# Loans of PSUM banks eight ticks apart, copies inside the next product, and another rule for ordering ScalarE, VectorE and GpSimd in a two-layer decoder

## Chip, core and metric

One core of a Trainium2 chip runs the whole program. The metric is the device time of one execution in microseconds (us). Engines are named as the profile names them: PE is TensorE (PEld its weight loads), DVE is VectorE, ACT is ScalarE, POOL is GpSimd, SP is SyncE, which issues most DMAs.

## What is computed

The reference runs 512 positions of width 1024, in float32, through two layers; each is followed by `x <- LayerNorm(alpha * x + sublayer(x))`.

```python
# even layer: one input projection feeds two branches
q, k, v, g_ret, xb, g_lru = split(x @ w_in)
ret = groupnorm(retention(rope(q), rope(k), v)) * silu(g_ret)     # 8 heads, chunks of 128
lru = rg_lru(conv4(xb)) * silu(g_lru)                             # gates, scan over positions
y = concat(ret, lru) @ w_out
# odd layer: differential attention, 8 heads, value width 256
q, k, v, g = split(x @ w_in)
w = softmax(q1 k1) - lam * softmax(q2 k2)                         # causal
y = (rmsnorm(w @ v) * silu(g)) @ w_out
```

## The kernel before

**Precision.** Each float32 operand of a product is split into a high part and a low remainder: ACT casts the high part, DVE subtracts it (`split`, L152 and L153). A product is then three matmuls, high by high (L156), low by high (L158) and high by low (L159), into one PSUM bank. So each weight tile of 128x1024 costs one ACT cast (`w53h`) and one DVE subtraction (`w53l`) behind its load; in the profile `w_r` is the raw tile.

**Stages.** The even layer's units run in the order of a list: gates (`gl`, `gr`), LRU inputs (`xb`), `q` and `k` per head, values (`ev`), and output products (`out`, `lo`, `ro`, `eo`) that add into `y` on DVE (L260, L262). `q` and `k` go through `rope`: three multiplications out of PSUM (L346, L349, L350), a sum (L351) and a split. Retention then multiplies keys by queries (`rs`), weights the scores (`rsd`, L475), multiplies by values (`ro`), and normalises (`rq`, `rv`, L497 to L508) into `retm`. The LRU branch goes through gate products (`pr`, `pi`), ACT functions with table loads (L528 to L544) and DVE rows up to a scan (L548) and L551 (`xc`), into `lrum`. At the end of the layer each block of 128 rows is normalised (`bst`, L371; L390, L392) and transposed on PE (`ht`, L615), and `hh` and `hl` are its two parts.

The odd layer computes values and gates of later groups together (`gates_values`): seven products of half blocks, some with weights and activations summed beforehand (`sx`), into two pairs of banks, `one` (`gv..a`) and `two` (`gv..b`). Between the products the banks are copied to SBUF (`p1`, `u`, `p7`).

**Order.** PE and SP keep the order of the code (`manual_schedule`). ACT, DVE and POOL are ordered by the scheduler from its own simulation of the program, with priorities given in the code (`high_priority(P_...)`). The side work, an attention block or a retention head, is a Python generator that is stepped by a clock, `side`: each call of `side.tick()`, after three matmuls of a main product, lets at most one such job go a step. A job yields the number of ticks to wait or a function that tells when. So the ticks set where the transposes (`wt`, L670), value products (`po`) and output transposes (L698) of an attention block stand in PE's order.

**Banks.** PSUM has four banks for main products (`ps_pj`), two for scores (`ps_sc`), one for `po` (`ps_av`) and one for transposes. An attention block takes `ps_av` for its value product, from there to the transposes of its result, plus `ATT_FREE` ticks. During `qk` units (`spare[0]` is true) it always borrows a bank of `ps_pj` instead, without a limit. The result `o` (L694) needs a square sum of `po` on ACT (L688) and a reciprocal root on POOL (L691, L363).

Of the kernel before, what the change touches and what calls it, by code (L numbers as in the profile page):

```python
# [34 lines left out]
ATT_TURN = (4, 3, 4, 4)  # L35
ATT_NORM = 5
ATT_VALUE, GV_VALUE = 2, 4
ATT_FREE = 2

P_ROPE, P_SCORES, P_SQUARE, P_GROUP, P_VALUE = 50, 13, 60, 5, 60  # L40
P_CONV, P_GATES = 9, 5
# [62 lines left out]
def trunk(ctx: ExitStack, tc: tile.TileContext, a):  # L104
    nc = tc.nc
    PS = bass.MemoryType.PSUM

    def pool(name, bufs, stack=ctx, **kw):
        return stack.enter_context(tc.tile_pool(name=name, bufs=bufs, **kw))
# [15 lines left out]
    side = Side()  # L125
    ALL = slice(None)

    def work(name):
        return wk.tile([P, S], F32, tag="wk", name=name)
# [4 lines left out]
    def bank(pl, tag, name):  # L134
        return pl.tile([P, 512], F32, tag=tag, name=name)
# [136 lines left out]
    for p in range(3):  # L272
        one, two = (2 * p, 2 * p + 1)
# [5 lines left out]
    for kind, i in ev:  # L279
        if kind in ("ro", "lo", "out"):  # L280
            order += [(eo[2 * i + j + n], None) for n in {"ro": (0,), "lo": (8,), "out": (8, 0)}[kind] for j in range(2)]
        else:
            n = 4 if kind == "v" else 1
# [9 lines left out]
    for kind, i in od:  # L293
        if kind == "o":
            order += [(oo[2 * hd + j], j) for hd in i for j in range(2)]
        elif kind == "gv":
# [3 lines left out]
            t = {n: [dram.tile([P, D], F32, tag=f"t{i}{n}{j}", name=f"t{i}{n}{j}") for j in range(2)] for n in (1, 2, 3, 4)}  # L300
# [104 lines left out]
    two = pool("two", 2, phase)  # L405
# [165 lines left out]
    for kind, i in ev:  # L571
# [18 lines left out]
        else:  # L590
            ps = t_unit(x, f"{kind}{i}")
# [53 lines left out]
    def attention(hd, qb, q, k, m):  # L645
        hc = (hd % 2) * 2 * P
        n = (qb + 1) * P
        ee = []
        z = small.tile([P, 2], F32, tag="z", name="z")
        for mp in range(2):  # L650
            ps = bank(ps_sc, "sc", f"as{hd}{mp}{qb}")
            mm3(ps[:, :n], cut(q[mp], ALL, slice(qb * P, qb * P + P)), cut(k[mp], ALL, slice(0, n)), True, True)
            with tc.high_priority(P_ATT):
                nm = small.tile([P, 1], F32, tag="nm", name="nm")
                nc.vector.tensor_tensor_reduce(out=ps[:, :n], in0=ps[:, :n], in1=mask[:, S - n:], scale=-QK_SCALE, scalar=3.0e38,  # L655
                                               op0=ALU.add, op1=ALU.min, accum_out=nm)
                e = es.tile([P, n], F32, tag=f"e{n}", name=f"e{hd}{mp}{qb}")
                nc.scalar.activation(out=e, in_=ps[:, :n], func=AF.Exp, scale=-1.0, bias=nm, accum_out=z[:, mp:mp + 1])  # L658
            ee.append(e)
        with tc.high_priority(P_ATT):  # L660

            zr = small.tile([P, 2], F32, tag="zr", name="zr")
            nc.vector.reciprocal(out=zr[:, 0:1], in_=z[:, 1:2])
            nc.vector.tensor_scalar(out=zr[:, 0:1], in0=zr[:, 0:1], scalar1=z[:, 0:1], scalar2=nlam, op0=ALU.mult, op1=ALU.mult)
            nc.gpsimd.tensor_scalar(out=zr[:, 1:2], in0=z[:, 0:1], scalar1=z[:, 0:1], scalar2=EPS, op0=ALU.mult, op1=ALU.mult)  # L665
            nc.vector.scalar_tensor_tensor(out=ee[0], in0=ee[1], scalar=zr[:, 0:1], in1=ee[0], op0=ALU.mult, op1=ALU.add)  # L666
        yield ATT_SCORES[qb] + busy[0]
        pt = bank(ps_tp, "tp", f"wt{hd}{qb}")
        for kb in range(qb + 1):
            nc.tensor.transpose(out=pt[:, kb * P:kb * P + P], in_=ee[0][:, kb * P:kb * P + P], identity=ident)  # L670
        with tc.high_priority(P_ATT):
            wt = part(n, f"w{hd}{qb}")
            split(pt[:, :n], wt)
        yield ATT_TURN[qb] + busy[0]

        here = lambda: max(vt.get(hd // 2, math.inf), 0 if spare[0] else av[0])
        if here() > side.now:
            yield here
        own = not spare[0]
        if own:  # L680
            av[0] = math.inf
        v = vs[hd // 2]
        po = bank(*(ps_av, "av") if own else (ps_pj, "pj"), f"po{hd}{qb}")
        for kb in range(qb + 1):
            mm3(po[:, :2 * P], cut(wt, ALL, slice(kb * P, kb * P + P)), cut(v[kb], ALL, slice(hc, hc + 2 * P)), kb == 0, kb == qb)
        with tc.high_priority(P_ATT):
            ss = small.tile([P, 1], F32, tag="ss", name="ss")
            nc.scalar.activation(out=po[:, 2 * P:], in_=po[:, :2 * P], func=AF.Square, scale=(2 * P) ** -0.5, accum_out=ss)  # L688
            rs = small.tile([P, 1], F32, tag="ars", name="ars")
            ve = small.tile([P, 1], F32, tag="rs", name="ave")  # L690
            nc.gpsimd.tensor_scalar(out=ve, in0=ss, scalar1=zr[:, 1:2], scalar2=None, op0=ALU.add)  # L691
            rsqrt(ve, rs)
            o = es.tile([P, 2 * P], F32, tag="o", name=f"o{hd}{qb}")
            nc.vector.scalar_tensor_tensor(out=o, in0=po[:, :2 * P], scalar=rs, in1=gates[qb, hd // 2][:, hc:hc + 2 * P], op0=ALU.mult, op1=ALU.mult)  # L694
        yield ATT_NORM + (not own)
        pm = po[:, 2 * P:]
        for i in range(2):
            nc.tensor.transpose(out=pm[:, i * P:i * P + P], in_=o[:, i * P:i * P + P], identity=ident)  # L698
        with tc.high_priority(P_ATT):
            split(pm.rearrange("p (i s) -> p i s", s=P), cut(m, ALL, ALL, slice(qb * P, qb * P + P)))  # L700

        if own:
            av[0] = side.now + ATT_FREE

    oj, om, vs, vt, av = {}, {}, {}, {}, [0]
# [59 lines left out]
    def load_sum(n, k):  # L765
        for j in range(2):
            nc.sync.dma_start(out=sx[:, k, :, 2 * j:2 * j + 2].bitcast(F32), in_=sd[n][:, :, 2 * j:2 * j + 2])
# [6 lines left out]
    def gates_values(i):  # L774
        def block(r, c):
            return lambda kt, n: cut(h, ALL, 4 * c + kt, slice((2 * r + n) * P, (2 * r + n) * P + P))

        def total(k):
            return lambda kt, n: tuple(sx[:, k, x, kt, n * P:n * P + P] for x in range(2))

        def product(ps, left, start, then=()):
            for j in range(2):
                if j and then:
                    load_sum(*then)
                w = take(3)
                for n in range(2):
                    for kt in range(2 * j, 2 * j + 2):
                        c = kt % 2 * HALF
                        mm3(ps[n], left(kt, n), cut(w, ALL, slice(c, c + HALF)), start and kt == 0, kt == KT // 2 - 1, skip_group_check=not start)
                        side.tick()  # L790

        def copies(ps, name):
            ts = [work(f"{name}{i}{n}") for n in range(2)]
            for t, p in zip(ts, ps):
                nc.scalar.copy(out=t, in_=p)
            return ts

        def gate(ps, ts, r):
            g = gp.tile([P, 2, S], F32, tag="g", name=f"og{i}{r}")
            for n in range(2):  # L800
                for hd in (2 * i - 2, 2 * i - 1):
                    side.need(oj[hd, 2 * r + n])
                gates[2 * r + n, i] = g[:, n]
            for n in range(2):
                nc.vector.tensor_tensor(out=g[:, n], in0=ps[n], in1=ts[n], op=ALU.add)
                silu2(g[:, n], g[:, n], ts[n])

        busy[0] = ATT_BUSY
        one = [bank(ps_pj, "pj", f"gv{i}a{n}") for n in range(2)]
        two = [bank(ps_pj, "pj", f"gv{i}b{n}") for n in range(2)]  # L810
        product(one, block(0, 0), True)
        p1 = copies(one, "p1")
        product(two, block(0, 1), True)
        gate(two, p1, 0)
        product(one, total(0), False)
        u = copies(one, "u")
        product(two, total(1), True, (0, 0))
        p7 = copies(two, "p7")
        product(one, total(0), False, (3, 1))
        past(i - 1)  # L820
        low = []
        for n in range(2):
            nc.vector.scalar_tensor_tensor(out=p7[n], in0=one[n], scalar=-1.0, in1=p7[n], op0=ALU.mult, op1=ALU.subtract)
            low.append(pair(vp, [P, S], "v", f"ov{i}{2 + n}"))
            split(p7[n], low[n])
        product(two, block(1, 1), False)
        gate(two, u, 1)
        product(one, total(1), False)
        for n in range(2):
            t = pair(vp, [P, S], "v", f"ov{i}{n}")  # L830
            nc.scalar.activation(out=t[0], in_=one[n], func=AF.Identity, scale=-1.0)
            nc.vector.scalar_tensor_tensor(out=t[1], in0=one[n], scalar=-1.0, in1=t[0].bitcast(F32), op0=ALU.mult, op1=ALU.subtract)
            vs.setdefault(i, []).append(t)
        vs[i] += low
        vt[i] = side.now + GV_VALUE
        busy[0] = 0
# [8 lines left out]
                for qb in range(SB):  # L845
                    side.need(oj[hd, qb])

    later, units, busy, spare = {}, 0, [0], [False]

    def swap_in():  # L850
        nonlocal sx
# [151 lines left out]
```

## Time and profile before

| | us |
|---|---|
| median of 3 runs | 929.88 |
| lowest to highest | 929.85 to 930.24 |
| profiled execution | 929.83 |
| its span, first to last instruction | 928.1 |
| PE busy in the span | 907.5 |
| DVE busy | 744.1 |
| ACT busy | 478.8 |

The profile gives each row of a timeline as start, duration, engine, line, operation, output and inputs with the buffer numbers left out, shapes, and in brackets the idle time of the engine before it with what ended it. The list of waits gives who waited for whom, the total, how often, and the longest. In the list of stages a row is a window in us, its length, the busy time of PE, PEld, DVE, ACT and POOL with the number of instructions, then the granted share of PE's clock, the DMA share and GB/s. The even layer runs to about 450 us, the odd layer from there.

### The profile page before, as it was taken

The numbers are of one execution on the slowest core, as the hardware profiler recorded it, in microseconds if no ns is written. First come the engines' busy times: TensorE is split into PE (matmuls) and PEld (weight loads), VectorE is DVE, ScalarE is ACT, GpSimd is POOL, SyncE is SP. The second block draws the span as 40 slices with busy tenths as digits, with TensorE's granted clock in tenths as the row PEclk, the third lists the DMA queues.
The fourth block names the chain that finished last, engine by engine and source line by source line (L and its number), as shares of the span: only waits on it lengthen the run. The fifth ranks groups of instructions, "written<-read, shape, count | busy, mean of one in ns | idle before, by whom it ended". The sixth has DMA issues, their size and how long they took to land.

```text
span 928.1 us, 11816 instructions
## 1 busy us (share of the span) xinstructions
PE 907.5 (98%) x4257; PEld 751.7 (81%) x4257; DVE 744.1 (80%) x1244; ACT 478.8 (52%) x779; POOL 103.0 (11%) x167
## 2 busy tenths in 40 slices
PE   9999999999999999999999999999999999999996
PEld 6888888887888878888888888888788888787885
DVE  5887987969768989897888997669867588877787
ACT  5467787556474668532434466333555334563340
POOL 0110010110101010010101120100200101101022
PEclk9999999999999999999999999999999999999998
DMA  7995463962929281525932127555247382286102
GB/s 250 295 295 148 127 180 91 273 171 66 284 61 278 82 206 63 192 87 176 342 130 70 65 79 261 204 204 182 91 133 270 123 293 90 69 274 242 52 1 90
DMA packets 46522, 152.92 MB, mean 165 GB/s; under 512 B 6144, under 2 KB 6272, under 8 KB 45696
## 3 DMA queue, kind: packets, MB, share of 16 engines
q1 hardware_dynamic: 41472, 135.39, 41.3%
q0 software_dynamic: 4992, 16.78, 9.3%
q8 instruction: 33, 0.54, 0.2%
q14 instruction: 25, 0.20, 0.1%
HBM read 139.57 MB, written 37.75 MB: 191 GB/s over the span
## 4 chain that ended last, share of the span: by engine, by line
PE 76%; DVE 13%; ACT 4%; issue 3%; POOL 2%; DMA 1%; SPq 0%; DVEq 0%; POOLq 0%; ACTq 0%
PE oo_ps L159 2%; PE oo_ps L156 2%; PE oo_ps L158 2%; PE out_ps L156 2%; PE out_ps L159 2%; PE out_ps L158 2%; PE gr_ps L159 1%; PE gr_ps L158 1%; PE gr_ps L156 1%; PE gl_ps L156 1%; PE gl_ps L159 1%; PE gl_ps L158 1%; PE xb_ps L158 1%; PE xb_ps L159 1%; PE xb_ps L156 1%
## 5 line engine op out<-in xcount | busy, mean ns | idle before, releaser
L658 ACT ACTIVATE e<-as,nm 128x128 f32<-128x128 f32 (+3 forms) x64 | 33.2, 524 | 39.6 <-DVE nm L655 39.5
L665 POOL TENSOR_SCALAR zr<-z 128x1 f32<-128x1 f32 x32 | 16.5, 516 | 272.0 <-ACT e L658 272.0
L694 DVE SCALAR_TENSOR_TENSOR o<-po,ars,og 128x256 f32<-128x256 f32 x32 | 15.5, 484 | 33.5 <-POOL ars L363 33.4
L187 POOL DMA_DIRECT2D t<-t x24 | 18.9, 786 | 156.0 <-DMA t<-in_od_w 151.0
L187 POOL DMA_DIRECT2D t<-in_od_w x24 | 19.1, 795 | 149.2 <-DMA t<-in_od_w 149.2
L655 DVE CUSTOM_DVE_ANT_0 as<-as,mask 128x128 f32<-128x128 f32 (+3 forms) x64 | 30.4, 508 | 2.2 <-PE as L159 2.0
L691 POOL TENSOR_SCALAR ave<-ss,zr 128x1 f32<-128x1 f32 x32 | 14.5, 454 | 126.3 <-ACT po L688 124.4
L688 ACT ACTIVATE po<-po 128x256 f32<-128x256 f32 x32 | 12.0, 375 | 27.1 <-PE po L159 24.7
L363 POOL TENSOR_TENSOR ars<-ave,nhalf 128x1 f32<-128x1 f32 x32 | 19.5, 610 | 2.7
L536 DVE TENSOR_TENSOR xbp<-xbp,xc 128x512 f32<-128x512 f32 x8 | 5.5, 692 | 17.6 <-ACT xbp L533 17.6
L666 DVE SCALAR_TENSOR_TENSOR e<-e,zr,e 128x128 f32<-128x128 f32 (+3 forms) x32 | 17.6, 550 | 0.9
L519 DVE SCALAR_TENSOR_TENSOR xc<-xbp,vecs,xc 128x509 f32<-128x509 f32 (+2 forms) x24 | 17.9, 744 | 0.1
L262 DVE TENSOR_TENSOR y<-oo_ps,y 128x512 f32<-128x512 f32 x24 | 16.0, 684 | 2.2 <-PE oo_ps L159 2.1
L475 DVE TENSOR_TENSOR rsd<-rs,dec 128x512 f32<-128x512 f32 (+3 forms) x32 | 15.5, 485 | 2.7 <-PE rs L159 2.7
L698 PE MATMUL po<-ident,o 128*128 128x128 f32 x64 | 12.3, 274 | 4.5 <-DVE o L694 4.5
L363 POOL TENSOR_TENSOR lrs<-lve,nhalf 128x1 f32<-128x1 f32 x8 | 7.3, 911 | 84.3 <-DVE lve L376 84.3
L698 PEld LDWEIGHTS po<-ident,o 128*128 128x128 f32 x64 | 8.7, 140 | 9.6 <-DVE o L694 5.7
L670 PE MATMUL wt<-ident,e 128*128 128x128 f32 x80 | 14.1, 275 | 0.0
L670 PEld LDWEIGHTS wt<-ident,e 128*128 128x128 f32 x80 | 10.7, 143 | 3.6 <-issue 0.2
L528 ACT ACTIVATE t<-pr,vecs 128x512 f32<-128x512 f32 x8 | 5.5, 688 | 15.0 <-PE pr L159 15.0
L152 ACT CAST hh<-ht 128x512 fp32r<-128x512 f32 x8 | 4.7, 588 | 15.5 <-PE ht L615 15.5
L658 ACT ACTIVATION_READ_ACCUMULATOR e<-as,nm 128x1 f32 x64 | 12.5, 195 | 0.0
(2846 smaller groups left out, 3470.3 us busy)
## 6 DMA issues: line engine op xcount, KB each, us to landing
w_r<-in_od_w SPq DMA_DIRECT2D x58, 512.0 KB, 5.8
w_r<-in_ev_w SPq DMA_DIRECT2D x47, 512.0 KB, 5.4
t<-in_od_w SPq DMA_DIRECT2D x48, 256.0 KB, 5.7
sx<-sd SPq DMA_DIRECT2D x24, 512.0 KB, 5.7
w_r<-t SPq DMA_DIRECT2D x24, 512.0 KB, 3.3
w_r<-in_ev_wo SPq DMA_DIRECT2D x16, 512.0 KB, 5.4
w_r<-in_od_wo SPq DMA_DIRECT2D x16, 512.0 KB, 4.4
t<-in_od_w POOLq DMA_DIRECT2D x24, 256.0 KB, 5.3
```

The lines of the kernel that those rows point to most:

```text
L156: nc.tensor.matmul(out=out, lhsT=l[0], rhs=r[0], start=start, stop=False, **kw)
L158: nc.tensor.matmul(out=out, lhsT=l[0], rhs=r[1], start=False, stop=False, **kw)
L159: nc.tensor.matmul(out=out, lhsT=l[1], rhs=r[0], start=False, stop=stop, **kw)
L187: nc.gpsimd.dma_start(out=dst, in_=two, max_dma_last_dim=4 * D, accum_op=ALU.add)
L363: nc.gpsimd.tensor_tensor(out=out, in0=var, in1=nhalf[:, :1], op=ALU.pow)
L519: nc.vector.scalar_tensor_tensor(out=xc[:, sh:], in0=xb[:, :S - sh], scalar=conv_w(w, c), in1=xc[:, sh:], op0=ALU.mult, op1=ALU.add)
L655: nc.vector.tensor_tensor_reduce(out=ps[:, :n], in0=ps[:, :n], in1=mask[:, S - n:], scale=-QK_SCALE, scalar=3.0e38, op0=ALU.add, op1=ALU.m ...
L658: nc.scalar.activation(out=e, in_=ps[:, :n], func=AF.Exp, scale=-1.0, bias=nm, accum_out=z[:, mp:mp + 1])
L665: nc.gpsimd.tensor_scalar(out=zr[:, 1:2], in0=z[:, 0:1], scalar1=z[:, 0:1], scalar2=EPS, op0=ALU.mult, op1=ALU.mult)
L666: nc.vector.scalar_tensor_tensor(out=ee[0], in0=ee[1], scalar=zr[:, 0:1], in1=ee[0], op0=ALU.mult, op1=ALU.add)
L670: nc.tensor.transpose(out=pt[:, kb * P:kb * P + P], in_=ee[0][:, kb * P:kb * P + P], identity=ident)
L698: nc.tensor.transpose(out=pm[:, i * P:i * P + P], in_=o[:, i * P:i * P + P], identity=ident)
```

## The change

Four things are changed. The scheduler orders ACT, DVE and POOL by its timeline simulation. A loan from `ps_pj` is possible only eight ticks after the last (`ATT_LENT`); until then, or whenever it is free, `ps_av` is taken. The copies of a pair of banks are issued within the next product, between its two halves, each held behind what was issued before on ACT. And during `gates_values` the transposes of `o` wait one tick more also for blocks in `ps_av`.

```diff
-ATT_FREE = 2
+ATT_FREE, ATT_LENT = 2, 8
...
-        here = lambda: max(vt.get(hd // 2, math.inf), 0 if spare[0] else av[0])
+        lent = lambda: (pj[0] + ATT_LENT) if spare[0] else math.inf
+        here = lambda: max(vt.get(hd // 2, math.inf), min(av[0], lent()))
         if here() > side.now:
             yield here
-        own = not spare[0]
+        own = lent() > side.now
         if own:
             av[0] = math.inf
+        else:
+            pj[0] = side.now
...
-        yield ATT_NORM + (not own)
+        yield ATT_NORM + max(not own, busy[0])
...
-        def product(ps, left, start, then=()):
+        def product(ps, left, start, then=lambda: None):
             for j in range(2):
-                if j and then:
-                    load_sum(*then)
+                if j:
+                    then()
...
-        def copies(ps, name):
-            ts = [work(f"{name}{i}{n}") for n in range(2)]
-            for t, p in zip(ts, ps):
-                nc.scalar.copy(out=t, in_=p)
-            return ts
+        def copies(ps, name, ts):
+
+            for n in range(2):
+                ts.append(work(f"{name}{i}{n}"))
+                tc.keep_in_program_order(nc.scalar.copy(out=ts[n], in_=ps[n]))
...
+        p1, u, p7, low = [], [], [], []
         product(one, block(0, 0), True)
-        p1 = copies(one, "p1")
-        product(two, block(0, 1), True)
+        product(two, block(0, 1), True, lambda: copies(one, "p1", p1))
         gate(two, p1, 0)
         product(one, total(0), False)
-        u = copies(one, "u")
-        product(two, total(1), True, (0, 0))
-        p7 = copies(two, "p7")
-        product(one, total(0), False, (3, 1))
+
+        def between():
+            load_sum(0, 0)
+            copies(one, "u", u)
+
+        product(two, total(1), True, between)
+
+        def between():
+            load_sum(3, 1)
+            copies(two, "p7", p7)
+
+        product(one, total(0), False, between)
         past(i - 1)
-        low = []
...
-    later, units, busy, spare = {}, 0, [0], [False]
+    later, units, busy, spare, pj = {}, 0, [0], [False], [0]
...
-    with tile.TileContext(nc) as tc:
+    with tile.TileContext(nc, schedule_with_timeline_sim=True) as tc:
```

Every engine has as many instructions as before, and ACT as many table loads. SP's order is the same. PE's is the same up to the attention of head 0. In `ps_pj`, `po60`, `po61` and `po62` took three banks in a row before, and `q71o` then took the bank of `q70o`; now `po61` is in `ps_av`, and `q71o` takes the bank that `gv3a0` left. `po31` and `po51` are in `ps_av` too. Some 300 of DVE's instructions and some 110 of ACT's stand elsewhere, most of them by a few places. Three pieces follow.

DVE in the even layer, at the rotary key of head 2 (`k_c`, `k_s`, `k2l`) between rows of the LRU branch (`t`, `r`, `xc`), of a retention norm (`rq`, `rsd`) and weight splits. Before:

```order
L346 TENSOR_TENSOR k_c<-k_ps,cos 128x512
L349 TENSOR_TENSOR k_s<-k_ps,sin 64x512
L545 SCALAR_TENSOR_TENSOR t_1146<-t_1146,xc_1062 128x512
L546 SCALAR_TENSOR_TENSOR r_1158<-r_1158,xc_1062 128x512
L350 TENSOR_TENSOR k_s<-k_ps,sin 64x512
L547 TENSOR_TENSOR r_1158<-r_1158,xbp_1060 128x512
L351 TENSOR_TENSOR k_c<-k_c,k_s 128x512
L548 SCALAR_TENSOR_TENSOR xc_1062<-t_1146,r_1158 128x512
L500 SCALAR_TENSOR_TENSOR rq_1187<-rv_1230,rq_1187 128x512
L551 TENSOR_TENSOR xc_1062<-xc_1062,gl_982 128x512
L153 TENSOR_TENSOR k2l<-k_c,k2h 128x512
```

Now:

```order
L545 SCALAR_TENSOR_TENSOR t_1146<-t_1146,xc_1062 128x512
L546 SCALAR_TENSOR_TENSOR r_1158<-r_1158,xc_1062 128x512
L346 TENSOR_TENSOR k_c<-k_ps,cos 128x512
L349 TENSOR_TENSOR k_s<-k_ps,sin 64x512
L350 TENSOR_TENSOR k_s<-k_ps,sin 64x512
L547 TENSOR_TENSOR r_1158<-r_1158,xbp_1060 128x512
L153 TENSOR_TENSOR w23l<-w_r,w23h 128x1024
L500 SCALAR_TENSOR_TENSOR rq_1187<-rv_1230,rq_1187 128x512
L351 TENSOR_TENSOR k_c<-k_c,k_s 128x512
L548 SCALAR_TENSOR_TENSOR xc_1062<-t_1146,r_1158 128x512
L501 SCALAR_TENSOR_TENSOR rsd_1233<-rq_1187,rsd_1233 128x512
L153 TENSOR_TENSOR w24l<-w_r,w24h 128x1024
```

L545 and L546 have moved ahead of the three multiplications of `k_c` and `k_s`, and `w23l` and `w24l` ahead of `k2l`; behind the last row shown stand L445 (`gl`), L551 (`xc`) and then `k2l`.

DVE later in the even layer, from the key of head 6 (`k_c`, `k_s`, `k6l`) to its neighbours, the LRU branch of block 6 (`t`, `r`, `xc`), the scores of head 5 (`rsd`, `r52l`) and the output additions (`y` from `lo_ps`). Before:

```order
L346 TENSOR_TENSOR k_c<-k_ps,cos 128x512
L349 TENSOR_TENSOR k_s<-k_ps,sin 64x512
L350 TENSOR_TENSOR k_s<-k_ps,sin 64x512
L542 SCALAR_TENSOR_TENSOR xc_2694<-t_2773,r_2785 128x512
L351 TENSOR_TENSOR k_c<-k_c,k_s 128x512
L543 SCALAR_TENSOR_TENSOR xc_2694<-xc_2694,r_2785 128x512
L153 TENSOR_TENSOR r52l<-rsd_2805,r52h 128x256
L153 TENSOR_TENSOR k6l<-k_c,k6h 128x512
```

Now:

```order
L542 SCALAR_TENSOR_TENSOR xc_2694<-t_2773,r_2785 128x512
L153 TENSOR_TENSOR q6l<-q_c,q6h 128x512
L153 TENSOR_TENSOR r52l<-rsd_2805,r52h 128x256
L543 SCALAR_TENSOR_TENSOR xc_2694<-xc_2694,r_2785 128x512
L346 TENSOR_TENSOR k_c<-k_ps,cos 128x512
L349 TENSOR_TENSOR k_s<-k_ps,sin 64x512
L350 TENSOR_TENSOR k_s<-k_ps,sin 64x512
L153 TENSOR_TENSOR w53l<-w_r,w53h 128x1024
L475 TENSOR_TENSOR rsd_2849<-rs_2845,dec_2549 128x128
L262 TENSOR_TENSOR y<-lo_ps_2840,y 128x512
L545 SCALAR_TENSOR_TENSOR t_2773<-t_2773,xc_2694 128x512
```

L542, `q6l`, `r52l` and L543 have moved ahead of `k_c`, and `w53l` and two output additions ahead of L351; `r53l` follows five rows after the last one shown.

ACT in the odd layer, around the copies of the first pair of `gv2` banks to `p` and the square of `po32` (the row with `ss`). Before:

```order
L658 ACTIVATE e_6155,z<-as_6149,nm 128x512
L658 ACTIVATE e_6163,z<-as_6157,nm 128x512
L795 COPY p_6197<-gv2a_6099 128x512
L795 COPY p_6198<-gv2a_6100 128x512
L152 CAST w116h<-w_r 128x1024
L688 ACTIVATE po_6179,ss<-po_6179 128x256
L152 CAST w117h<-w_r 128x1024
```

Now, where L691 and L799 are the former L688 and L795:

```order
L658 ACTIVATE e_6155,z<-as_6149,nm 128x512
L152 CAST w116h<-w_r 128x1024
L658 ACTIVATE e_6163,z<-as_6157,nm 128x512
L691 ACTIVATE po_6188,ss<-po_6188 128x256
L799 COPY p_6215<-gv2a_6099 128x512
L799 COPY p_6217<-gv2a_6100 128x512
L152 CAST w117h<-w_r 128x1024
```

The square has moved from behind the two copies to ahead of them. Beside this, ACT's cast of `w102`, which stood behind the softmax rows of `po21`'s block and the square of `po21`, now stands ahead of those rows, and so does `w128` at `po41`.

## Prediction

> **What bounds the kernel now.** I read the page's head first, then TensorE's list of waits, then the timeline around the places where the change moves rows. Two lines of the page's head: the span, and busy time by engine.
>
> ```profile
> span 928.1 us, 11816 instructions
> ...
> PE 907.5 (98%) x4257; PEld 751.7 (81%) x4257; DVE 744.1 (80%) x1244; ACT 478.8 (52%) x779; POOL 103.0 (11%) x167
> ```
>
> TensorE (PE) is busy for 907.5 of 928.1 us, so 20.6 us is all that any reordering can win, and the change removes no matmul. The list of PE's waits names most of what lies inside the kernel: columns are who waited for whom, us in total, times, longest.
>
> ```profile
> PE po L698 <- DVE o L694: 4.5, 3, 1.9
> PE q71o_ps L156 <- DVE q70o_s L350: 2.2, 1, 2.2
> PE ro L158 <- DVE r63l L153: 1.2, 1, 1.2
> ```
>
> Every wait in it ends at VectorE (DVE) or behind it: PE is fed by VectorE, which is 80% busy. A program whose PE has no slack and whose VectorE has little loses whatever is put ahead of the row that PE wants next. The profiled execution took 929.83 us, its span 928.1; the median of the runs is 929.88, so the sum below, made against 929.8, may be read against either. About 0.2%, 1.9 us, is what a measurement can tell from no change.
>
> **The change, first part: the even layer (up to 450 us).** There the matmuls and SyncE's loads keep their order; only ScalarE and VectorE are reordered, with the same instructions and the same number of table loads. Busy time stays, so the cost is in waits alone, and I price each place by its rows. First k2, the key of head 2. VectorE's and PE's timeline before:
>
> ```profile
> 126.21 0.69 DVE L346 TENSOR_TENSOR k_c<-k_ps,cos 128x512 f32<-128x512 f32 x1
> ...
> 128.00 0.69 DVE L545 SCALAR_TENSOR_TENSOR t<-t,xc 128x512 f32<-128x512 f32 x1 [0.40 <-ACT r L544]
> ...
> 133.57 0.68 DVE L153 TENSOR_TENSOR k2l<-k_c,k2h 128x512 fp32r<-128x512 f32 x1
> 134.17 0.69 DVE L501 SCALAR_TENSOR_TENSOR rsd<-rq,rsd 128x512 f32<-128x512 f32 x1
> 134.78 1.22 DVE L153 TENSOR_TENSOR w23l<-w_r,w23h 128x1024 fp32r<-128x1024 f32 x1
> ```
>
> ```profile
> 135.32 0.40 PE L159 MATMUL rs<-q2h,k2l 128*128 128x512 f32 x1
> ```
>
> The starts give the step: 0.60 us for 512 columns (133.57 to 134.17, some 0.08 under the duration), and by the same overlap 1.13 to 1.14 for a weight split or a scan of 1.22. k2l was ready at 134.25, 1.07 before PE read it. Now t and r (L545, L546) stand ahead of k_c, and t waits for ScalarE's r until 128.00: k_c starts at 128.00 + 2 x 0.61 = 129.2. From k_c to k2l stand nine rows of 0.60, the scan L548 and two weight splits of 1.13: 5.5 + 3.4 = 8.9. k2l starts at 138.1 and ends at 138.8: PE waits 3.4 us where it waited none.
>
> Next k6, whose PSUM bank PE takes for lo_ps, and r53l, which PE already waited for. The same views:
>
> ```profile
> 308.67 1.28 ACT L540 ACT_TABLE_LOAD   x1
> 309.96 0.63 ACT L540 ACTIVATE r<-t 128x512 f32<-128x512 f32 x1
> ```
>
> ```profile
> 312.46 0.68 DVE L350 TENSOR_TENSOR k_s<-k_ps,sin 64x512 f32<-64x512 f32 x1
> 313.18 0.69 DVE L542 SCALAR_TENSOR_TENSOR xc<-t,r 128x512 f32<-128x512 f32 x1
> ```
>
> ```profile
> 315.32 0.39 PE L156 MATMUL lo_ps<-w49h,lrum2h 128*128 128x512 f32 x1
> ...
> 318.87 0.33 PE L158 MATMUL ro<-r53l,ev13h 128*128 128x128 f32 x1 [0.38 <-DVE r53l L153]
> ```
>
> L542, which could start at 313.18 and hardly sooner, now stands with q6l, r52l and L543 ahead of k_c: k_c starts at 313.2 + 3 x 0.60 + 0.34 = 315.3, and k_s, two rows on, ends at 315.3 + 2 x 0.60 + 0.68 = 317.2 (before: 313.14). PE wanted the bank at 315.32: with the semaphore's 0.05, 2.0 us. Behind that, w53l, a small product, three y additions, t, r and L351 stand ahead of r53l: 1.13 + 0.2 + 6 x 0.60 after 317.2 gives 322.1, ending 0.3 later at 322.4. PE, already 2.0 late, would want it at 320.5 (318.87 - 0.38 + 2.0): 1.9, of which 0.38 was there before, so 1.5 more.
>
> ScalarE has one more table load in that chain (and one less elsewhere), priced at 1.28 by the row above, after which the ACTIVATE starts at once (308.67 + 1.28 = 309.95). [...]
>
> Three more places of this kind, each as VectorE's row and then PE's:
>
> ```profile
> 64.76 0.69 DVE L153 TENSOR_TENSOR k0l<-k_c,k0h 128x512 fp32r<-128x512 f32 x1
> ...
> 386.41 0.68 DVE L508 TENSOR_TENSOR rq<-rq,gr 128x512 f32<-128x512 f32 x1
> ...
> 411.92 1.41 DVE L392 SCALAR_TENSOR_TENSOR y<-y,lrs,ln 128x512 f32<-128x512 f32 x2
> ```
>
> ```profile
> 67.65 0.40 PE L159 MATMUL rs<-q0h,k0l 128*128 128x512 f32 x1
> ...
> 389.40 0.39 PE L156 MATMUL eo_ps<-w63h,retm3h 128*128 128x512 f32 x1
> ...
> 414.45 0.60 PE L615 MATMUL ht<-ident,y 128*128 128x128 f32 x4
> ```
>
> Ahead of k0l now stand L547, the scan, w14l, gl and L551: 3 x 0.60 + 2 x 1.13 = 4.1, so it ends at 69.5: 1.9. Ahead of L508, which makes the last retention output, stand two y additions, w63l and w65l, 3.5: it ends at 390.5, the cast of 0.62 follows, PE gets retm3h at 391.2 and its low part some 0.3 later; with the two lambda rows that also moved ahead I take 2.3. Ahead of L392 of the third row block stand bst, a y addition, w69l, an hl and w70l: 3 x 0.60 + 2 x 1.13 = 4.1; its first half ends at 416.7 against 414.45: 2.3.
>
> At the start, vc of the first value block freed the bank of PE's first gate product:
>
> ```profile
> 27.39 0.69 DVE L457 TENSOR_TENSOR vc<-ev_ps,vm 128x512 f32<-128x512 f32 x1
> ```
>
> ```profile
> 29.69 0.39 PE L156 MATMUL gl_ps<-xh,w4h 128*128 128x512 f32 x1
> ```
>
> w6l, gw0l and w7l now precede it: 2 x 1.13 + 0.60 = 2.9, plus the wait for w6's load, against 1.6 to spare: I take 2.0 net of the earlier w3l; 0 to 4, as it hangs on when the weights land.
>
> These make 3.4 + 2.0 + 1.5 + 1.9 + 2.3 + 2.3 + 2.0 = 15.4. Smaller ones of the same form (k1 and xc2, k7, two y banks) I estimate from one or two rows of 0.60 or 1.13 each with under 1 us to spare: 3.5, between 0 and 6. The wait for r63l (1.2) goes, since r63h and r63l are now ahead of w57. Even layer: 15.4 + 3.5 - 1.2 = +17.7.
>
> **Second part: the odd layer, where banks, copies and order act together.** q71o waited 2.2 us because po60, po61 and po62 all borrowed a bank of ps_pj in a row, so that q71o got the bank of q70o, still being read. With eight ticks between loans po61 stays in ps_av, q71o gets a bank that the products before it left, and the wait goes. What is late next there is k70o, which takes q70o's bank a whole unit (24 matmuls) later: covered. Of the 4.5 us that po's transposes waited for o in three waits, the longest, 1.9, is in the gv2 product, and the gv3 product has its twin; ScalarE and PE before, at gv2:
>
> ```profile
> 668.84 1.07 ACT L795 COPY p<-gv2a 128x512 f32<-128x512 f32 x2
> 669.79 1.08 ACT L152 CAST w116h<-w_r 128x1024 fp32r<-128x1024 f32 x1
> ```
>
> ```profile
> 673.51 0.44 PE L698 MATMUL po<-ident,o 128*128 128x128 f32 x2 [1.94 <-DVE o L694]
> ```
>
> The two copies went ahead of po32's square and delayed it by about 0.95; now they are recorded half a product later and stand behind it. Beside that, the transposes come one tick (three matmuls, 0.68) and six score matmuls (0.65) later. 0.95 + 1.3 against 1.94: gone, and so are the twin and the third, 4.5 in all. If the square is not earlier, 0.6 stays at each of the long ones. The copies' own readers, gate and the p7 update, come a product later; half a product, 12 matmuls or 2.7 us, still covers two copies. The cover to watch: copies of a bank end before PE overwrites it one product on.
>
> The wait in gv2 also cost clock. The stages behind it and behind its twin in gv3, with the granted clock third from the end:
>
> ```profile
> 674.00:678.00 4.00, 4.00 (x17) 3.40 (x16) 2.86 (x9) 1.80 (x6) 0.27 (x1) 0.57 0.00 0
> 800.00:804.00 4.00, 3.37 (x21) 2.98 (x22) 3.44 (x9) 1.82 (x7) 0.32 (x2) 1.00 0.00 0
> ```
>
> 4 us at 0.57 is 1.7 us lost, after one of the two. So the odd layer wins 4.5 + 2.2 + 1.7 = 8.4. Against it, the order puts the cast of w102 (and w128) ahead of the softmax rows in front of po21 (po41):
>
> ```profile
> 593.86 1.05 ACT L152 CAST w102h<-w_r 128x1024 fp32r<-128x1024 f32 x1
> ```
>
> 0.95 on ScalarE and about as much on VectorE for its split, 1.9 together, of which PE's slack may take none or all: I take 1.0 at each of two places. po31 and po51, now in ps_av, have their transposes a tick earlier: 0.5 each; e603, now behind the om6l splits, 1.1; three smaller ones 0.8. That is 4.9 (0 to 7). Odd layer: 4.9 - 8.4 = -3.5. GpSimd's stores of one activation sum move ahead of two others, long before SyncE loads them back: nothing.
>
> Sum: 929.8 + 17.7 - 3.5 = 944.0. The new waits include five of 2 us or more; the trace has the clock cooled after one such wait and not after another, and q71o's 2.2 is a third: I add 1.7 for one of the five: **945.7**.
>
> **The rivals.** *The moved rows fall into VectorE's idle fifth, and the waits won are all that counts.* For it: 184 us of VectorE idle. It decides at k2: if k_c runs before t's wait ends, or k2l ends before 135.3, the even layer costs nothing. Then 929.8 - 8.4 - 1.2 + half of the odd costs (2.5) = 922.7, faster. Against it: at 128.00 VectorE stood idle for 0.40 us behind a waiting t with its next rows queued: none passed it. 0.09.
>
> *Each wait lets VectorE catch up, so the next ones shrink by half*: 929.8 + 9 - 3.5 = 935.3. Against it: PE's rows at these places, from 29.69 to 414.45, lie 25 to 180 us apart, time enough to be level again before the next. 0.18.
>
> *Each of the five long waits cools the clock*: 944.0 + 5 x 1.7 = 952.5. For it the 0.57, against it the 1.00. [...] 0.15.
>
> *Gains and costs cancel*: within 1.9 us. 0.05.
>
> **How the numbers follow.** The forecast, 945.7, has 0.53. Faster 0.09, same 0.05, slower 0.86. The range goes from the halved case to beyond the cooled one, with the start's and the smaller places' bounds: 935 to 956.
>
> **What would show it.** In the changed profile's waits of PE: rs for k2l with about 3 us near 139, lo_ps for k6's bank and ro for r53l near 320, rs for k0l near 69, eo_ps for retm3, ht for y; and no q71o, no po wait of 1.9. If these even-layer waits are missing, the forecast is wrong from its first term; if they stand and the time is under 936, it is their size.

## The result, and the profile after

| | us |
|---|---|
| before, median of 4 runs beside it | 929.87 (928.46 to 930.24) |
| changed, median of 4 runs | 956.11 (953.15 to 958.88) |
| ratio | 1.0288, 95% interval 1.0267 to 1.0308 |
| changed, profiled execution; its span; granted clock | 953.15; 951.4; 0.991 |

The change costs 26.2 us, or 23.3 between the two profiled executions. The forecast was 945.7 with a range of 935 to 956: its direction held, but the median lies 0.1 us above the range's end. The head of the changed page and its list of PE's waits answer to those of before:

```profile
span 951.4 us, 11865 instructions
...
PE 917.3 (96%) x4257; PEld 755.1 (79%) x4257; DVE 745.4 (78%) x1244; ACT 481.5 (51%) x779; POOL 96.1 (10%) x167
```

```profile
PE po L701 <- DVE o L697: 4.3, 5, 1.1
PE rs L159 <- DVE k2l L153: 3.3, 1, 3.3
PE eo_ps L156 <- ACT retm3h L152: 2.5, 1, 2.5
PE lo_ps L156 <- DVE k_s L350: 2.1, 1, 2.1
PE ro L158 <- DVE r53l L153: 2.0, 1, 2.0
PE rs L159 <- DVE k0l L153: 1.8, 1, 1.8
PE wt L670 <- DVE e L666: 1.7, 3, 1.2
PE gl_ps L156 <- DVE vc L457: 1.6, 1, 1.6
PE ht L615 <- issue: 1.2, 1, 1.2
PE rs L156 <- ACT k7h L152: 1.2, 1, 1.2
```

VectorE is as busy as before (745.4 against 744.1) and the number of matmuls is the same, yet PE is busy for 9.8 us more: a first sign that some of the same work ran at a slower clock (by the windows below, 5.1 of it). The waits are the named ones. At k2, VectorE and then PE:

```profile
134.61 0.69 DVE L545 SCALAR_TENSOR_TENSOR t<-t,xc 128x512 f32<-128x512 f32 x1 [2.57 <-ACT r L544]
...
135.82 0.69 DVE L346 TENSOR_TENSOR k_c<-k_ps,cos 128x512 f32<-128x512 f32 x1
...
144.94 0.69 DVE L153 TENSOR_TENSOR k2l<-k_c,k2h 128x512 fp32r<-128x512 f32 x1
```

```profile
145.68 0.50 PE L159 MATMUL rs<-q2h,k2l 128*128 128x512 f32 x1 [3.27 <-DVE k2l L153]
```

VectorE stood idle for 2.57 us behind t with k_c queued, as the forecast's walk had it, and from k_c to k2l it took 9.1 us where 8.9 was worked out. At k6, L542 again waits ahead of k_c, k_s ends late, and r53l is behind all of it:

```profile
327.64 0.69 DVE L542 SCALAR_TENSOR_TENSOR xc<-t,r 128x512 f32<-128x512 f32 x1 [0.85 <-ACT r L541]
...
331.19 0.68 DVE L350 TENSOR_TENSOR k_s<-k_ps,sin 64x512 f32<-64x512 f32 x1
...
336.85 0.28 DVE L153 TENSOR_TENSOR r53l<-rsd,r53h 128x128 fp32r<-128x128 f32 x1
```

```profile
331.93 0.50 PE L156 MATMUL lo_ps<-w49h,lrum2h 128*128 128x512 f32 x1 [2.10 <-DVE k_s L350]
...
337.19 0.33 PE L158 MATMUL ro<-r53l,ev13h 128*128 128x128 f32 x1 [1.96 <-DVE r53l L153]
```

What the waits did to the clock is read from the list of stages, cut where the clock changes (the granted share stands third from the end, PE's busy time first after the length). The stretches at half clock are 3.41 us long, and the rows are cut at that length from where they begin and end. One such row is called a window here, one at half clock a cooled window. Around k0l's wait, in the changed kernel:

```profile
64.78:68.19 3.41, 3.41 (x17) 2.83 (x16) 3.38 (x6) 2.61 (x3) 0.00 (x0) 1.00 0.83 141
68.19:71.60 3.41, 1.62 (x7) 0.75 (x5) 3.38 (x5) 1.44 (x3) 0.78 (x1) 1.00 0.41 167
71.60:75.02 3.42, 3.40 (x8) 2.75 (x9) 2.08 (x3) 0.64 (x2) 0.00 (x1) 0.50 0.49 77
```

In the second row PE is idle for 1.79 of 3.41 us, and the third is at half clock: 1.7 us lost, the 1.7 that the prediction had read off as 0.57 over 4 us. There are four such windows in this execution, behind k0l, k2l, r53l and retm3h, where before had one. By the starts of the same matmul in both traces, the changed kernel is 26.6 us late at the even layer's end and 24.1 at the last product. With 1.7 for each window that is 19.8 of waits in the even layer, and in the odd one -2.5, of which -1.7 is before's window that is gone.

### The profile page after: what moved, and what is told of

It is laid out like the page before. It is cut to its first block, busy times and chain, and to the rows that moved or that the text cites. A ratio compares the mean times of both kernels' runs of the same rounds, so it can differ in the third digit from the quotient of the medians.

```text
span 951.4 us, 11865 instructions
## 1 busy us (share of the span) xinstructions
PE 917.3 (96%) x4257; PEld 755.1 (79%) x4257; DVE 745.4 (78%) x1244; ACT 481.5 (51%) x779; POOL 96.1 (10%) x167
## 4 chain that ended last, share of the span: by engine, by line
PE 59%; DVE 21%; ACT 10%; DMA 5%; issue 4%; SPq 0%; POOL 0%; DVEq 0%; ACTq 0%
PE oo_ps L159 2%; PE oo_ps L156 2%; PE oo_ps L158 2%; DMA w_r<-t 2%; DMA w_r<-in_od_w 2%; DMA w_r<-in_ev_w 1%; PE gr_ps L156 1%; PE gr_ps L159 1%; PE gr_ps L158 1%; PE gl_ps L156 1%; PE q_ps L156 1%; PE q_ps L159 1%; PE gl_ps L158 1%; PE q_ps L158 1%; PE gl_ps L159 1%
## 5 line engine op out<-in xcount | busy, mean ns | idle before, releaser
L665 POOL TENSOR_SCALAR zr<-z 128x1 f32<-128x1 f32 x32 | 13.0, 405 | 265.4 <-ACT e L658 265.4
L697 DVE SCALAR_TENSOR_TENSOR o<-po,ars,og 128x256 f32<-128x256 f32 x32 | 15.4, 482 | 20.0 <-POOL ars L363 19.8
L691 ACT ACTIVATE po<-po 128x256 f32<-128x256 f32 x32 | 11.9, 371 | 31.1 <-PE po L159 30.8
L694 POOL TENSOR_SCALAR ave<-ss,zr 128x1 f32<-128x1 f32 x32 | 11.0, 343 | 135.2 <-ACT po L691 118.5
L346 DVE TENSOR_TENSOR q_c<-q_ps,cos 128x512 f32<-128x512 f32 x8 | 5.5, 689 | 11.0 <-PE q_ps L159 11.0
```

## The experiments

All run on one chip per group, against the kernel before in the same group.

**Which part costs.** The first four take the change apart. The old rule with the other two parts (the kernel is the changed one but for this line):

```diff
-    with tile.TileContext(nc, schedule_with_timeline_sim=True) as tc:
+    with tile.TileContext(nc) as tc:
```

> The change without the timeline simulation: banks lent every eight ticks and copies inside the next product, under the old ordering rule. If the ordering rule is the whole loss and the other parts win as the odd layer's own rows say (po waits 4.5 and q71o 2.2 gone, some 1.0 of new waits at po31 and po51, and the 1.7 us of cooled clock behind po32's wait gone): about 929.9 - 7.4 = 922.5, with no wait over 1.2 us on TensorE in the even layer. Rival, that the banks and the copies carry part of the loss: 930 or more. Rival, that the waits only move to other transposes, as the changed profile's po list (4.3 us in five waits) suggests: 925 to 928.

Measured: 926.36 (925.80 to 927.00), ratio 0.9962 (0.9949 to 0.9976), clock of the profiled one 0.998. The first entries of PE's waits in it:

```profile
PE po L701 <- DVE o L697: 1.8, 4, 0.5
PE ro L158 <- DVE r63l L153: 1.2, 1, 1.2
```

So banks and copies together win 3.9 us, with no half-clock window inside the program. It is the third expectation: some of the wait moves to other transposes and to splits (om1l, ov10l, w33l, w53l, 0.3 to 0.5 each). This version is faster than both kernels.

The rule alone, on the kernel before:

```diff
-    with tile.TileContext(nc) as tc:
+    with tile.TileContext(nc, schedule_with_timeline_sim=True) as tc:
```

> The kernel before with the timeline simulation alone. If the rule is the whole loss: the even layer as in the changed kernel (waits for k0l, k2l, lo_ps, r53l, retm3h; end of the layer later by 26 us, 6.8 of which is cooled clock), and the odd layer without the gains of the other two parts, so some 3 to 5 us above the changed kernel: 957 to 961. Rival, that the three parts only lose together: within 2 us of the kernel before.

Measured: 955.63 (954.77 to 959.65), ratio 1.0290 (1.0268 to 1.0311). The even layer's waits come back to within 0.1 us, but for the start's (1.80 against 1.57), and the even layer ends 26.5 us late. The rule is the whole loss. The time lies 1.4 under the first expectation: q71o's 2.2 is there again, but po's waits are 2.6 in all, against 4.3 with banks and copies changed as well. So under the new rule those two bring next to nothing (a ratio of 1.0290 without them, 1.0288 with them), under the old one 3.9.

The banks alone (old rule, copies as before):

```diff
+        lent = lambda: (pj[0] + ATT_LENT) if spare[0] else math.inf
+        here = lambda: max(vt.get(hd // 2, math.inf), min(av[0], lent()))
...
+        yield ATT_NORM + max(not own, busy[0])
```

> Only the loans eight ticks apart (and the one tick more before the transposes), old rule, copies as before. q71o's wait of 2.2 goes, the two waits of 1.9 in gv2 and gv3 shrink by a tick (0.7 each), po31 and po51 add 0.5 each: 929.9 - 2.2 - 1.4 + 1.0 = 927.3; one cooled window (1.7) can go as well or stay. Rival, that the loan limit moves the wait to other units: no change within 1.9.

Measured: 927.42 (927.10 to 927.77), ratio 0.9969 (0.9957 to 0.9981): as expected, with q71o gone and po's longest wait down to 0.8. No cooled window is left inside the program (clock 0.998, before 0.996).

The copies alone (old rule, banks as before):

```diff
+        product(two, block(0, 1), True, lambda: copies(one, "p1", p1))
```

> Only the copies half a product later, old rule, loans as before. The square of po32 and po52 is 0.95 earlier, so the two waits of 1.9 fall to about 1.0 each and neither cools the clock: 929.9 - 1.9 - 1.7 = 926.3; q71o's 2.2 stays. Rival, that what reads the copies becomes late: 930 to 932.

Measured: 929.43 (927.14 to 932.13), ratio 0.9998 (0.9985 to 1.0011): nothing. The waits and ScalarE at gv2 in it:

```profile
PE po L698 <- DVE o L694: 4.0, 3, 1.9
PE q71o_ps L156 <- DVE q70o_s L350: 2.2, 1, 2.2
```

```profile
668.64 1.07 ACT L796 COPY p<-gv2a 128x512 f32<-128x512 f32 x2
...
670.53 0.40 ACT L688 ACTIVATE po<-po 128x256 f32<-128x256 f32 x1
```

Here the copies stay ahead of the square of po32, though they are recorded later. Being held behind what was recorded before them does not hold them behind what comes after. With the banks changed as well, under the same old rule, the square does come first; ScalarE in the first experiment:

```profile
672.54 0.37 ACT L691 ACTIVATE po<-po 128x256 f32<-128x256 f32 x1
...
672.93 1.06 ACT L799 COPY p<-gv2a 128x512 f32<-128x512 f32 x2
```

Why the banks decide this was not traced. It is worth little: with the banks alone the square still stands behind the copies (673.13 against 671.24), and PE does not wait ahead of po32's transposes there either. The copies beside the banks bring 1.1 us by the medians (926.36 against 927.42), with intervals that overlap.

**What the waits cost beyond themselves.** The changed kernel, with the warm-up's matmuls put ahead of the five long waits. They write a bank that nobody reads:

```diff
+            ps = bank(ps_sc, "sc", f"rs{h}{jb}")
+            fill({(0, 0): 6, (2, 0): 12}.get((h, jb), 0))
```

> The changed kernel with matmuls that add nothing to the result (the warm-up's, 0.227 us each) put on TensorE ahead of the five long waits: 6 before k0's scores, 12 before k2's, 7 at lo_ps, 7 before r53, 9 at retm3. They take TensorE's waiting time and no other. If cooled clock is what was left out of the forecast: no half-clock window in the middle of the program, span about 951.4 - 6.8 = 944.6, time 946.4, and the runs within some 1.5 us of each other. Rival, that the even layer's waits themselves are longer than was priced: 953 or more, spread as before. Rival, that the matmuls delay the rows behind them: above 948.

Measured: 950.78 (949.67 to 952.22), ratio 1.0210 (1.0190 to 1.0229). No half-clock window at the five places (clock of the profiled one 0.997, against 0.991), and 5.3 us won by the medians (7 by the ratios), with the rows that PE waits for as late as before: at k2l, 12 matmuls of 0.227 and 0.85 of idle, where it was 3.27 of idle. The time is still 4.4 above what was expected: the profiled one has a wait of 1.98 at the start (1.57 in the changed kernel), and 2.13 at the third row block's transposes (1.20 in the changed kernel), with a window behind it.

With fewer of them:

```diff
-            fill({(0, 0): 6, (2, 0): 12}.get((h, jb), 0))
+            fill({(0, 0): 2, (2, 0): 8}.get((h, jb), 0))
```

> The same with fewer matmuls (2, 8, 3, 2, 5), so that each of the five waits keeps 1.3 to 1.5 us of idle. [...] Rival, that every idle time brings a proportional chance of a cooled window: one or two windows remain, 948 to 950.

Measured: 956.23 (955.07 to 957.82). Again no window at the five places, where 1.3 to 1.8 us of idle is left, so none of the rival's one or two; but the time is that of the changed kernel: at a granted clock of 0.993 the trace has 3.83 us of wait at the start and 3.56 at the transposes, with one and two cooled windows behind them. So there was something that the five places don't account for; why the transposes' wait grew was not traced.

The first five fills with two more, at those places:

```diff
+        fill(8 if name == "gl0" else 0)
...
+                fill(6 if (sb, hf) == (2, 0) else 0)
```

> The changed kernel with the five fills of the first one and two more, at the two places where the runs since showed waits over 1.8 us: 8 matmuls ahead of the first gate product (gl_ps, 1.6 to 3.8 us from execution to execution) and 6 ahead of the third row block's transposes (ht). If windows of half clock are what lies between the changed profile's 944.6 (span less four windows of 1.7) and the runs: no such window, 946.4 to 948.5 (the start's wait still depends on when the weights land), and a spread of 2 us at most. Rival, that waits of changing length make the spread: 950 or more, with a spread of 4 us.

Measured: 950.93 (950.21 to 952.63), ratio 1.0221 (1.0202 to 1.0240), clock 0.995 to 0.996. The spread, 2.4 us, is near the 2 that were expected; the time is the rival's. The profiled execution (clock 0.996) has one cooled window, behind a wait of 2.2 us for o at 622 us, where nothing was filled. With the clock at 0.995 to 0.996, waits of changing length are left. At the start, 8 matmuls of 0.227 and 2.26 of idle make 4.1 us.

The kernel before with fills at its own three waits:

```diff
+        fill(6 if name == "q71o" else 0)
...
+        fill(6 if (hd, qb) in ((3, 2), (5, 2)) else 0)
```

> The kernel before with 6 such matmuls ahead of each of its three waits of about 2 us (the transposes of po32 and po52, and q71o). TensorE waits as long as before for its work. If its spread of 5 us comes from none to three windows of half clock: the lowest times of the kernel before, 928 (span 926.4), in every run, so about 2 us under its median of 930.3 to 931.3. Rival, that the clock has no part in it: 930 to 931, spread as before.

Measured: 929.33 (928.66 to 930.45), ratio 0.9991 (0.9978 to 1.0005), where the kernel before beside it ran from 926.98 to 933.92. The spread goes from 6.9 to 1.8 us, and no run falls under 0.997 in granted clock; the median moves by 0.8, less than half of what was expected, and the interval holds 1, so no change of the time is shown. In the 20 runs of the kernel before that stand beside the first four experiments, time follows the clock: 0.997 and 0.998 go with 927.76 to 928.63, 0.992 with 932.79, some 5 us apart, which is three windows of 1.7. In the 17 runs beside this experiment the order is the same but less clean: 0.997 goes with 926.98 to 929.96, 0.992 with 933.29 and 933.92.

**One place put right.** The changed kernel with block 2's t, r, scan and xc held behind k2l (`split.last`, which is k2l's row there):

```diff
+                with tc.issue_after(split.last):
+                    scan()
+                    end()
```

> The changed kernel with one place put right: the rows of the LRU branch of block 2 (t, r, scan, xc) are held behind k2l. If the rows ahead of k_c make k2's wait: k2l is ready before TensorE wants it, the wait of 3.3 goes, with it its cooled window (1.7 in nearly every execution): 956.1 - 5.0 = 951, the other four long waits unchanged. Rival, that the lost time comes back at the next place that the held rows feed: 954 or more.

Measured: 954.23 (952.19 to 955.55), ratio 1.0249 (1.0230 to 1.0267). VectorE, and PE's matmul, which now waits for nothing:

```profile
142.85 0.68 DVE L153 TENSOR_TENSOR k2l<-k_c,k2h 128x512 fp32r<-128x512 f32 x1
143.45 0.68 DVE L546 SCALAR_TENSOR_TENSOR t<-t,xc 128x512 f32<-128x512 f32 x1
```

```profile
143.61 0.48 PE L159 MATMUL rs<-q2h,k2l 128*128 128x512 f32 x1
...
157.93 0.49 PE L156 MATMUL pr<-xc3h,gw2h 128*128 128x512 f32 x1 [0.90 <-ACT xc3h L152]
159.23 0.50 PE L158 MATMUL pr<-xc3l,gw2h 128*128 128x512 f32 x1 [0.80 <-DVE xc3l L153]
```

Both expectations hold in part. At 149.7 us the trace is 5.0 us earlier against the changed kernel's than it was ahead of the place (3.3 of wait and 1.7 of clock), and 11 us further on 2.0 is back, in waits for xc3, which the changed kernel hasn't: the held rows now stand between k2l and the rows that make xc3.

**The same kernel again**, one execution:

> The changed kernel once more, one execution with its trace. [...] Rival, that the length of a wait alone decides: the same four windows.

Measured: 957.92, granted clock 0.987 where the first execution has 0.991, six cooled windows (behind gl_ps, two behind k2l, r53l, retm3h, and po at 750 us), none behind k0l. So the rival is out. The waits inside the even layer are the same to 0.03 us, but for the start's; po's at 750 us is 2.04 against 1.00. First the stages around k0l in the kernel with the rule alone, where k0l's wait, 1.8 us as well, lay in two windows, with 1.56 and 0.25 us of idle in them, and the clock stayed at 1.00:

```profile
68.18:71.59 3.41, 1.85 (x8) 0.94 (x6) 3.41 (x5) 1.44 (x3) 0.00 (x0) 1.00 0.64 235
71.59:75.01 3.42, 3.17 (x14) 2.63 (x15) 2.18 (x4) 1.66 (x3) 0.78 (x1) 1.00 0.48 75
```

and the start and k2's two windows in the second execution of the changed kernel:

```profile
30.16:33.57 3.41, 0.63 (x3) 0.57 (x4) 3.41 (x10) 2.33 (x4) 1.57 (x2) 1.00 1.01 326
33.57:36.98 3.41, 3.41 (x10) 2.66 (x9) 3.41 (x7) 0.48 (x1) 0.00 (x0) 0.50 1.08 321
...
142.80:146.21 3.41, 1.16 (x4) 0.30 (x3) 3.41 (x5) 0.43 (x1) 0.27 (x1) 1.00 0.52 207
146.21:149.63 3.42, 2.35 (x6) 1.87 (x7) 3.38 (x7) 1.18 (x2) 0.51 (x1) 0.50 0.90 259
149.63:153.03 3.40, 3.40 (x10) 2.63 (x9) 1.61 (x3) 1.55 (x4) 0.00 (x0) 0.50 0.26 53
```

The start's wait is 3.15 against 1.57. ScalarE, VectorE and PE there, in the first execution and in the second:

```profile
23.86 1.05 ACT L152 CAST w6h<-w_r 128x1024 fp32r<-128x1024 f32 x1 [1.11 <-DMA w_r<-in_ev_w]
...
31.39 0.47 PE L156 MATMUL gl_ps<-xh,w4h 128*128 128x512 f32 x1 [1.57 <-DVE vc L457]
```

```profile
26.59 1.05 ACT L152 CAST w6h<-w_r 128x1024 fp32r<-128x1024 f32 x1 [3.06 <-DMA w_r<-in_ev_w]
...
27.67 1.22 DVE L153 TENSOR_TENSOR w6l<-w_r,w6h 128x1024 fp32r<-128x1024 f32 x1 [1.80 <-ACT w6h L152]
...
32.12 1.28 DVE L457 TENSOR_TENSOR vc<-ev_ps,vm 128x512 f32<-128x512 f32 x2
...
32.94 0.47 PE L156 MATMUL gl_ps<-xh,w4h 128*128 128x512 f32 x1 [3.15 <-DVE vc L457]
```

w6 landed 2.7 us later, and with w6l ahead of vc on VectorE that reaches PE. The kernel before cast w6h later still, and lost nothing by it, since vc stood ahead:

```profile
27.81 1.05 ACT L152 CAST w6h<-w_r 128x1024 fp32r<-128x1024 f32 x1 [4.28 <-DMA w_r<-in_ev_w]
```

So the start was put right by itself: the splits of w6, gw0 and w7 are held behind the first vc (of the edit, the lines for w6 and w7):

```diff
+                with tc.issue_after(vcs[0]) if n in (6, 7) else ExitStack():
+                    split(raw[:, c], cut(w, ALL, c), scale=scale)
```

> The changed kernel with the start put right: the splits of w6, gw0 and w7 held behind the first value block's vc. w6's cast began between 23.9 and 26.6 us in two executions of the changed kernel, so a w6l ahead of vc hands the landing of a weight to TensorE. If that wait is what lifts the median above the changed profile: the gl_ps wait of 1.6 to 3.2 us goes, with its window in most executions, and the other four long waits stay: 956.1 - 2.8 - 1.2 = 952. Rival, that TensorE waits as long one row later: 955 or more.

Measured: 950.71 (948.01 to 952.71), ratio 1.0226 (1.0201 to 1.0250). The start's wait is gone, and 5.4 us with it by the medians, where 4 were expected. These are four runs each, which spread over 5.7 and 4.7 us; the intervals of the two ratios don't overlap, so a gain is shown, its size only roughly.

This edit and the fills together (at k0, k2, lo_ps, r53, retm3 and the transposes):

> Both together: the start put right, and the fills at k0, k2, lo_ps, r53, retm3 and the third transposes. If waits and windows of half clock are all there is above 944.6 less the start's 1.6: 943.0 + 1.75 of launch + about 0.2 for each of six fills = 946, with no half-clock window and a spread of 2 us. Rival, that something else holds the time up: 949 or more.

Measured: 946.62 (945.30 to 947.78), ratio 1.0180 (1.0161 to 1.0199), as expected but for one window in the profiled one, behind two waits for k7h and k7l together (1.59 us). From 956.1, by the medians, the start's wait and its window take 5.4, the other windows about 4.1 (950.71 - 946.62); what is left, 946.6, is the new waits as waits.

## Why the prediction was wrong

**The even layer's waits were right.** Step by step, forecast and then the changed profile: k2l 3.4 and 3.27; k6's bank 2.0 and 2.10; r53l 1.5 more and 1.58 more; k0l 1.9 and 1.81; retm3 2.3 and 2.50; the transposes 2.3 and 1.20; the start 2.0 and 1.57; the smaller ones 3.5 and 3.5 (k7, xc2, two y banks); r63l -1.2 and gone. In all 17.7 (the transposes came to half of their price), against 16.3 in the list of waits and 19.8 by the matmuls' starts: besides its idle time, k2l's wait costs 0.17 (its matmul starts 3.44 us later than back to back, with 3.27 of idle) and k0l's as much (1.98, with 1.81), which by an estimate from these two is 2 for a dozen waits; where the last 1.5 comes from is open. The rival that the moved rows fall into VectorE's idle time is out by k2's rows, and the halved waits by the sum.

**The odd layer came out near, by another way.** Forecast -3.5, measured -2.5. q71o's wait and before's window are gone. The step on the copies, whose 0.95 was to come from being recorded later, was not what did it. Alone they aren't moved by that and win nothing (fourth experiment); under the new rule alone both start ahead of the square (693.75 and 695.34 against 697.43), and po32's transposes still wait only 0.16. Under the old rule po's waits of 1.9 go by the banks and the tick (third experiment). And the rule gives back at po what they win: 4.3 us in five waits, where the same banks and copies have 1.8 under the old rule. That the sum came near is in part luck.

**The step that failed is the clock's term, one window of 1.7 for five waits.** The trace had a window behind one wait of 1.94 and none behind its twin of 1.93 or q71o's 2.19, and the prediction took that as odds of about one in five and kept the many windows as a rival, at 952.5 with a chance of 0.15. The runs show four windows in one execution and six in another, against one of before: 5.1 and 8.5 us more, where the forecast had none net. Of the 7.5 us between the forecast and the profiled execution, 5.1 are this term (6.8 where 1.7 was put), 2.1 the even layer's waits (19.8 against 17.7) and 1.0 the odd layer (-2.5 against -3.5); 0.8 is won behind the last product. The twins in before differ by where they lay: one whole inside a window, the other with its last 0.13 us beyond the window's end.

```profile
670.79:674.21 3.42, 1.48 (x8) 0.98 (x7) 2.57 (x4) 1.61 (x5) 1.51 (x2) 1.00 0.45 153
674.21:677.62 3.41, 3.41 (x13) 2.84 (x13) 2.42 (x8) 1.59 (x6) 0.27 (x1) 0.50 0.00 0
...
797.09:800.50 3.41, 1.60 (x8) 0.98 (x6) 2.52 (x5) 2.21 (x4) 1.51 (x2) 1.00 0.43 154
800.50:803.92 3.42, 3.29 (x21) 2.90 (x22) 2.94 (x9) 1.74 (x7) 0.27 (x1) 1.00 0.00 0
```

Behind the first window, with 1.94 us of idle in it, the next is at half clock; behind the other, with 1.81, it is not. Of the six waits of 1.8 to 2.2 us in the two traces, of before and of the first execution of the changed kernel, three had a cooled window behind them (1.94 for po32, 1.81 for k0l, 1.96 for r53l) and three had none (the twin's 1.93, q71o's 2.19, 2.10 for k6's bank). q71o's 2.19 lay in two windows, with 1.51 and 0.68 us of idle in them, the 2.10 in two with 1.18 and 0.91. So even odds are the estimate for a wait of about 2 us, from three of six, not one in five. k2's 3.3 had one cooled window behind it in the first execution of the changed kernel and two in the second.

The second part of the miss is the start. The prediction priced it at 2.0, between 0 and 4, "as it hangs on when the weights land", which is what it did (1.57 and 3.15 in two executions); but a wait whose length changes cools a window in some executions (3.15 in the second) and not in others (1.57 in the first), and the two together made 5.4 us by the medians, with the spreads named above. The range's end of 956 had no room for both: 952.5 with 2.0 more at the start and 2.5 more at the smaller places, the bounds that the prediction itself gave, is 957.0.

## What to carry to other kernels

Where PE is the bound, price a wait of 2 us as the wait and, for half of such waits (the three of six above), 1.7 us of clock besides; by that estimate five of them are a term of some 4 to 5 us, not a remainder. When a scheduler reorders an engine in its own simulated time, look for rows that wait on a table load or on a weight's landing and now stand ahead of a row that PE wants next: VectorE hands that wait on, as in its 2.57 us of idle at k2 with k_c queued. Take a change of several parts apart on the chip early: here two parts won 3.9 us, and the third hid that behind a loss of 26.

## What the runs showed of the hardware

Between the warm-up and the last product, the clock of before and of the changed kernel's first execution was granted in full but for one stretch of 3.41 us at half clock in the one and four in the other. In the second execution of the changed kernel one of them, behind k2, lasted 6.82. In the first one the stretches of full clock between the four are 71.68, 187.73 and 71.68 us long, which is 21, 55 and 21 times 3.41.

In rows of 3.41 us cut from each trace's own boundaries, the next row was at half clock behind 1.94 us of PE idle (before), 1.79, 2.40, 1.96 and 2.50 (the changed kernel), 2.78 and 2.25 (its second execution, at gl_ps and k2) and 1.59 (the start put right, with fills). It was at full clock behind 1.81 and 1.51 (before) and 1.56 (the rule alone). So the idle time in the row does not by itself tell which it will be: 1.59 and 1.79 are on the one side and 1.81 on the other. Of the rows at half clock, the one behind k2 in the second execution had another 1.07 of idle in it and was followed by one more; the one of before and the four of the changed kernel, with 0.02 or less, were not.

With the waits inside the even layer equal to 0.03 us, the changed kernel had four cooled windows in one execution and six in another. The kernel before ranges over 3.7 to 6.9 us in groups of 9 to 20 runs, at 1.7 each the worth of two to four windows, and kernels without a wait over 1.3 us in them over 0.7 (the banks alone, 8 runs) and 1.2 (the old rule, 5 runs).

With matmuls that compute nothing issued in the five long waits, the granted clock of the profiled execution was 0.997, against 0.991, with no cooled window behind them: 5 to 7 us of the changed kernel's time (956.11 to 950.78 by the medians), with the rows that PE waited for as late as before.
